# The first microseconds of an encoder trunk: copies of the row selectors queued on VectorE behind the first head's row parts, and mask transfers to device memory queued behind GpSimd's other masks

## The chip, the cores and the metric

One core of one Trainium2 chip runs the whole program. The metric is the device time of one execution in microseconds (us); a run's figure is the median of several executions, and the profile is of one further execution. TensorE (PE) multiplies matrices, VectorE (DVE), ScalarE (ACT) and GpSimd (POOL) work element by element, SyncE (SP) issues most of the DMA transfers. Each engine works through its own queue in order; it waits at the head of that queue until what the instruction needs is there.

## The reference

Two residual layers, each a token mixer and a squared-ReLU MLP; layer 0 mixes with a bidirectional gated DeltaNet of 8 heads, layer 1 with a bidirectional GLA of 4 heads. 512 tokens of width 1024. The change touches only the start of layer 0:

```python
def _mixer_gdn(h, w_in, conv_w, a_log, dt_bias, norm_g, w_out):
    proj = jnp.matmul(h, w_in).astype(F32)
    qkv = jax.nn.silu(_depthwise_conv(proj[..., :A_CONV_CH], conv_w.astype(F32)))
    z = proj[..., A_CONV_CH:A_CONV_CH + A_VW]
    ba = proj[..., A_CONV_CH + A_VW:].reshape(bn, s, 2, 2, A_HEADS)
    q = _l2norm(heads(qkv[..., :A_W], A_DK)) * (A_DK ** -0.5)
    k = _l2norm(heads(qkv[..., A_W:2 * A_W], A_DK))
    v = heads(qkv[..., 2 * A_W:], A_DV)
    beta = jax.nn.sigmoid(ba[:, :, 0]).transpose(2, 0, 3, 1)
    g = (-jnp.exp(a_log) * jax.nn.softplus(ba[:, :, 1] + dt_bias)).transpose(2, 0, 3, 1)
    o_f = _gated_delta_chunked(q, k, v, beta[0], g[0])
    o_b = _flip(_gated_delta_chunked(_flip(q), _flip(k), _flip(v), _flip(beta[1]), _flip(g[1])))
    ...
```

Within a chunk the delta rule needs `exp(gc[i] - gc[j])` for all pairs of rows i, j of the chunk (`gc` is the running sum of `g`), masked to one triangle per direction, and the inverse of a unit triangular matrix built from it.

## The kernel before

**Tiling.** The 512 tokens are four blocks of 128 (`NT` = 4), the width is eight blocks (`KT` = 8). Products keep fp32 accuracy by splitting each operand into a high and a low part: ScalarE casts the high part (`wh`, `xth`; L102), VectorE subtracts to get the low part (`wl`, `xtl`; L107), and TensorE does three products per block of the width (L128, L129, L130). A projection of one head (`pjk`, `pjq`, `pjv`, `pjz`) is thus 24 matmuls of 128x128 by 128x512. Weights come into three rotating buffers `wst`; the split parts also have three buffers.

**Stages.** `gates` projects the gate columns (`bap`) and the key of head 0 (`pjk`) as the first blocks of x arrive, after 42 transposes without use, then computes log decays on VectorE: a chain of small operations on tiles `gd`, `ge`, `gl`, `gy` (L1295 to L1313). `masks` has GpSimd build the constant masks. Then the heads run as a pipeline: each round gives head i-2 its recurrence (`recur`), head i-1 its solve (`solve`) and head i its projections (`project`).

**Head 0.** `project` ends each of k, q, v with a five-tap convolution (`conv`): one ScalarE product (L1418) and four VectorE operations (L1422). When k and q are done, ScalarE loads the table for SiLU, applies it to both (L1465), loads the former table again (L57), and TensorE transposes k, then q, into one bank (`ktp`, L1489), from which ScalarE takes sums of squares (`junk`, L1494). From their logarithm `lnr` and from `gc` VectorE forms the row parts `rw` and `rsp` (L1505, L1546, L1547), TensorE turns them into rows (`rtp`, L1550, copied to `rt`), and for head 0 alone `spread_by_products` spreads these rows over 128 partitions by a product with the two selectors `sel` (`ep`, L1560). A selector is a 4x128 tile; GpSimd makes both in `sf` (named `self`, L1181 to L1183) and VectorE casts them (L1187). Later heads spread their rows through device memory instead: SP fills the tile `E` with the masks `laterd` (L1470), and GpSimd's queue adds the rows (L1539). `laterd` is written once, by four transfers that GpSimd issues (L1194).

**What sets the order.** A scheduler at build time puts the instructions of each engine in an order, by estimated durations and by the order of the code; `issue_after(x)` places what is written under it behind instruction x. At run time the order of an engine is fixed. The tiles `yr`, `gl`, `self` and `E` of the heads take turns in the two buffers of tag "E", so head 1's `E` may be filled only when the selectors have been read from `self`.

Of the kernel before, what the change touches and what calls it, by code (L numbers as in the profile page):

```python
# [8 lines left out]
F32 = mybir.dt.float32  # L9
F32R = mybir.dt.float32r  # L10
# [3 lines left out]
ALU = mybir.AluOpType  # L14
# [3 lines left out]
P = 128  # L18
# [3 lines left out]
NT = S // P  # L22
# [884 lines left out]
class GlaHead:  # L907


    def __init__(self, c, pool, h, w_in, consts, masks, oth, otl):  # L910
        self.c, self.pool, self.h, (self.w_in, self.w_vr) = c, pool, h, w_in
        self.consts, self.masks, self.oth, self.otl = consts, masks, oth, otl
# [210 lines left out]
NEG = -1e30  # L1123


class GdnConst:
# [47 lines left out]
    def masks(self):  # L1174
        c, pool = self.c, self.pool
        G = c.nc.gpsimd
        self.idh = pool.tile([P, P], F16, name="idh", bufs=1)
        G.tensor_copy(self.idh, c.ident)

        sf = pool.tile([4, 2, P], F32, name="self", tag="E", bufs=2)  # L1180
        G.memset(sf, 0.0)  # L1181
        for s in range(2):
            G.affine_select(out=sf, in_=sf, compare_op=ALU.not_equal, fill=1.0, base=-2 * s,  # L1183
                            pattern=[[-1, 2], [0, P]], channel_multiplier=1)
        self.sel = [pool.tile([4, P], F32R, name=f"sel{d}", tag="vn", bufs=9) for d in range(2)]
        for d in range(2):
            c.nc.vector.tensor_copy(self.sel[d], sf[:, d, :])  # L1187

        self.after = later = pool.tile([P, 2, P], F32, name="later", bufs=1)
        for d in range(2):  # L1190
            self.tri(later[:, d, :], d, False, 0.0, NEG)
        self.later = self.dram.tile([P, 2, NT, P], F32, name="laterd", bufs=1)
        for n in range(NT):
            G.dma_start(self.later[:, :, n, :], later)  # L1194

        self.nd = pool.tile([P, P], F32, name="nd", bufs=1)
        G.tensor_scalar(self.nd, c.ident, -1.0, 1.0, ALU.mult, ALU.add)

        self.same4 = pool.tile([P, P], F16, name="same4", bufs=1)
        self.off = {}  # L1200
        prev = None
        for w in (4, 8, 16, 32):
            f = pool.tile([P, P], F32, name="blk", tag="cf", bufs=2)
            G.memset(f, 1.0)
            fv = f.rearrange("p (a b) -> p a b", b=w)
            G.affine_select(out=fv, in_=fv, compare_op=ALU.is_ge, fill=0.0, base=0,
                            pattern=[[-w, P // w], [0, w]], channel_multiplier=1)
            G.affine_select(out=fv, in_=fv, compare_op=ALU.is_ge, fill=0.0, base=w - 1,
                            pattern=[[w, P // w], [0, w]], channel_multiplier=-1)
            if w == 4:  # L1210
                G.tensor_copy(self.same4, f)
            else:
                m = pool.tile([P, NT, P], F16, name=f"off{w // 2}", bufs=1)
                G.tensor_tensor(m, f.unsqueeze(1).to_broadcast([P, NT, P]), prev.unsqueeze(1).to_broadcast([P, NT, P]),
                                ALU.subtract)
                self.off[w // 2] = m
            prev = f

        ic = pool.tile([P, P // 4, 4], F32, name="ic", tag="cf", bufs=2)
        G.tensor_copy(ic, c.ident.rearrange("p (b c) -> p b c", c=4))  # L1220
        n = P // 4
        while n > 1:
            n //= 2
            G.tensor_tensor(ic[:, :n, :], ic[:, :n, :], ic[:, n:2 * n, :], ALU.add)
        self.ic = pool.tile([P, 4], F16, name="icc", bufs=1)
        G.tensor_copy(self.ic, ic[:, 0, :])

    @contextlib.contextmanager
    def then(self):
# [164 lines left out]
class GdnHead:  # L1394
# [146 lines left out]

    def turn_rows(self, rw):

        c, V = self.c, self.c.nc.vector
        rs = c.small.tile([P, NT, 4], F32R, name="rsp", tag="rsp")
        V.tensor_copy(rs[:, :, 0:2], rw)  # L1546
        V.tensor_tensor(rs[:, :, 2:4], rw, rs[:, :, 0:2].bitcast(F32), ALU.subtract)  # L1547
        rtp = self.bank("rtp", tag="tp")
        for n in range(NT):
            c.nc.tensor.transpose(rtp[:4, n, :], rs[:, n, :].bitcast(F32), c.ident)  # L1550
        self.rt = self.pool.tile([4, S], F32R, name="rt0", tag="on", bufs=2)
        c.nc.scalar.copy(self.rt, rtp[:4, :, :].rearrange("p n i -> p (n i)"))
# [340 lines left out]
```

## Time and profile before

| what | value |
|---|---|
| median of 3 runs | 1319.1 us (1318.91 to 1319.72) |
| the profiled execution | 1320.66 us, its span 1319.0 us, mean granted TensorE clock 0.995 |
| busy: TensorE / VectorE / ScalarE / GpSimd | 1295.5 / 1105.9 / 803.8 / 136.5 us |
| DMA | 165.92 MB, mean 126 GB/s |

In the rows of a timeline the columns are start in us, duration in us, engine, line, operation, tile written from tiles read, shape, count; in brackets how long the engine stood idle before the row and what released it. Rows can overlap, since an engine starts one before the last has drained. The group and queue lines carry their own labels. SPq, POOLq and PEq are the queues' own steps, such as issuing a transfer.

### The profile page before, as it was taken

The page shows a single profiled execution, that of the slowest core. Times are in us where ns is not written, and L with a number is a line of the kernel's source. Part 1 is how long each engine was busy: PE and PEld are TensorE (multiplying, and loading weights), DVE is VectorE, ACT ScalarE, POOL GpSimd, SP SyncE. Part 2 cuts the span into 40 slices and gives each one's busy share as a digit, 9 for nine tenths or more (in the row PEclk, how much of TensorE's full clock was granted, in tenths as well). Part 3 has the DMA queues.
Part 4 walks back from the last instruction along what each step waited for, and adds up shares of the span by engine and source line. Part 5 has one row for each costly group of instructions (what it writes and reads, how often), then busy time and mean ns, then how long its engine had stood idle before and what let it go on. Part 6 is the DMA issues. An engine that isn't in the chain of part 4 may idle for free.

```text
span 1319.0 us, 22255 instructions
## 1 busy us (share of the span) xinstructions
PE 1295.5 (98%) x8608; PEld 1110.9 (84%) x8608; DVE 1105.9 (84%) x1789; ACT 803.8 (61%) x1598; POOL 136.5 (10%) x190
## 2 busy tenths in 40 slices
PE   9999999999999999999999999999999999999996
PEld 7778888788877899999998888888889899989985
DVE  6788889878868989989988787867879789899987
ACT  4567676777633666656667754554466566566656
POOL 6000000000001810101101100000001001101021
PEclk9899999999999999999999999999999999999998
DMA  5233223332422575476547521211216276556565
GB/s 198 81 112 97 62 84 98 97 97 75 134 84 95 179 155 191 116 213 169 147 152 160 154 81 63 81 48 64 97 65 224 80 208 161 143 176 134 172 142 143
DMA packets 47373, 165.92 MB, mean 126 GB/s; under 512 B 5875, under 2 KB 6307, under 8 KB 47267
## 3 DMA queue, kind: packets, MB, share of 16 engines
q1 hardware_dynamic: 33171, 114.52, 25.7%
q0 software_dynamic: 13984, 49.95, 18.6%
q8 instruction: 67, 1.10, 0.3%
q14 instruction: 39, 0.32, 0.1%
q10 hardware_dynamic: 112, 0.03, 0.0%
HBM read 125.00 MB, written 2.65 MB: 97 GB/s over the span
## 4 chain that ended last, share of the span: by engine, by line
PE 85%; DVE 5%; ACT 4%; DMA 2%; issue 2%; POOL 1%; SPq 0%; DVEq 0%; ACTq 0%; POOLq 0%
PE pjv L128 3%; PE pjv L129 3%; PE pjv L130 3%; PE pX L130 3%; PE pX L129 3%; PE pX L128 3%; PE m L1755 3%; PE fx L130 3%; PE fx L128 3%; PE fx L129 3%; PE fyz L128 2%; PE fyz L130 2%; PE fyz L129 2%; PE pj L130 2%; PE pj L129 2%; PE scp L1008 2%
## 5 line engine op out<-in xcount | busy, mean ns | idle before, releaser
L102 ACT CAST wh<-wst 128x1024 fp32r<-128x1024 f32 x152 | 159.6, 1050 | 107.4 <-PE fyz L129 27.9
L107 DVE TENSOR_TENSOR wl<-wst,wh 128x1024 fp32r<-128x1024 f32 x150 | 184.3, 1231 | 41.5 <-ACT wh L102 41.1
L107 DVE TENSOR_TENSOR w2l<-w2r,w2h 128x1024 fp32r<-128x1024 f32 x92 | 111.4, 1221 | 21.4 <-ACT w2h L102 21.4
L102 ACT CAST w2h<-w2r 128x1024 fp32r<-128x1024 f32 x94 | 98.4, 1048 | 42.3 <-DMA w2r<-w2r 25.1
L415 POOL DMA_DIRECT2D w2r<-w2r x56 | 47.9, 887 | 494.2 <-DVE w2l L107 278.8
L464 DVE TENSOR_TENSOR wst<-wst 128x512 f32<-128x512 f32 x120 | 80.0, 686 | 0.8
L102 ACT CAST ah<-h 128x1024 fp32r<-128x1024 f32 x56 | 58.8, 1050 | 30.2 <-PE pY L129 11.5
L107 DVE TENSOR_TENSOR al<-h,ah 128x1024 fp32r<-128x1024 f32 x56 | 68.3, 1220 | 6.6 <-ACT ah L102 6.6
L130 PE MATMUL pX<-w2h,al 128*128 128x512 f32 x168 | 66.3, 394 | 0.0
L129 PE MATMUL pX<-w2l,ah 128*128 128x512 f32 x168 | 65.9, 392 | 0.0
L128 PE MATMUL pX<-w2h,ah 128*128 128x512 f32 x168 | 65.5, 390 | 0.0
L128 PE MATMUL pjv<-wh,xth 128*128 128x512 f32 x128 | 54.8, 428 | 0.0
L130 PE MATMUL fyz<-xh,wl 128*128 128x256 f32 x192 | 53.5, 279 | 0.0
L130 PE MATMUL fx<-xth,wl 128*128 128x256 f32 x192 | 53.4, 278 | 0.0
L128 PE MATMUL fyz<-xh,wh 128*128 128x256 f32 x192 | 53.4, 278 | 0.0
L128 PE MATMUL fx<-xth,wh 128*128 128x256 f32 x192 | 53.2, 277 | 0.0
L130 PE MATMUL fx<-xh,wl 128*128 128x256 f32 x192 | 53.2, 277 | 0.0
L128 PE MATMUL fx<-xh,wh 128*128 128x256 f32 x192 | 53.2, 277 | 0.0
L129 PE MATMUL fyz<-xl,wh 128*128 128x256 f32 x192 | 53.2, 277 | 0.0
L129 PE MATMUL fx<-xtl,wh 128*128 128x256 f32 x192 | 53.1, 277 | 0.0
L129 PE MATMUL fx<-xl,wh 128*128 128x256 f32 x192 | 53.1, 277 | 0.0
L129 PE MATMUL pj<-xtl,wh 128*128 128x256 f32 (+1 forms) x160 | 52.0, 326 | 0.2 <-DVE xtl L194 0.2
(540 smaller groups left out, 4318.4 us busy)
## 6 DMA issues: line engine op xcount, KB each, us to landing
wst<-in_w SPq DMA_DIRECT2D x68, 512.0 KB, 4.6
w2r<-in_w SPq DMA_DIRECT2D x60, 512.0 KB, 4.5
w2r<-w2r POOLq DMA_DIRECT2D x56, 512.0 KB, 5.8
wst<-in_a_in SPq DMA_DIRECT2D x32, 512.0 KB, 4.2
wst<-in_b_vr SPq DMA_DIRECT2D x16, 512.0 KB, 3.4
wst<-in_a_out SPq DMA_DIRECT2D x8, 512.0 KB, 4.4
wst<-in_b_in SPq DMA_DIRECT2D x8, 512.0 KB, 3.5
wst<-in_b_out SPq DMA_DIRECT2D x8, 512.0 KB, 3.2
```

The source lines that it names most:

```text
L102: h = nc.scalar.copy(hi, src)
L107: self.halves = h, nc.vector.tensor_tensor(lo, src, hi.bitcast(F32), ALU.subtract)
L128: mm(ps, ah, bh, start=start, stop=False, **kw)
L129: mm(ps, ah, bl, start=False, stop=False, **kw)
L130: self.last_mm = mm(ps, al, bh, start=False, stop=stop, **kw)
L415: nc.gpsimd.dma_start(blocks[a + (q,)], blocks[b + (q,)], accum_op=ALU.add)
L464: plus = lambda a, b: V.tensor_tensor(a, a, b, ALU.add)
L1008: T.matmul(ps[:, n, :], kh[:, sl], qh[:, sl], start=True, stop=True)
L1755: T.matmul(ps[:, d, :], *ops(d), start=True, stop=True)
```

## The change

The making of `sf` and of the `later` masks moves to the end of `masks`, behind all other masks, and the four transfers to `laterd` are placed behind the last operation on `sf`. The two casts of the selectors leave `masks` and go to `turn_rows` of head 0, behind the second row part.

```diff
@@ masks
         self.idh = pool.tile([P, P], F16, name="idh", bufs=1)
         G.tensor_copy(self.idh, c.ident)
 
-        sf = pool.tile([4, 2, P], F32, name="self", tag="E", bufs=2)
-        G.memset(sf, 0.0)
-        for s in range(2):
-            G.affine_select(out=sf, in_=sf, compare_op=ALU.not_equal, fill=1.0, base=-2 * s,
-                            pattern=[[-1, 2], [0, P]], channel_multiplier=1)
-        self.sel = [pool.tile([4, P], F32R, name=f"sel{d}", tag="vn", bufs=9) for d in range(2)]
-        for d in range(2):
-            c.nc.vector.tensor_copy(self.sel[d], sf[:, d, :])
-
-        self.after = later = pool.tile([P, 2, P], F32, name="later", bufs=1)
-        for d in range(2):
-            self.tri(later[:, d, :], d, False, 0.0, NEG)
-        self.later = self.dram.tile([P, 2, NT, P], F32, name="laterd", bufs=1)
-        for n in range(NT):
-            G.dma_start(self.later[:, :, n, :], later)
-
         self.nd = pool.tile([P, P], F32, name="nd", bufs=1)
...
         G.tensor_copy(self.ic, ic[:, 0, :])
+
+        sf = pool.tile([4, 2, P], F32, name="self", tag="E", bufs=2)
+        G.memset(sf, 0.0)
+        for s in range(2):
+            made = G.affine_select(out=sf, in_=sf, compare_op=ALU.not_equal, fill=1.0, base=-2 * s,
+                                   pattern=[[-1, 2], [0, P]], channel_multiplier=1)
+        self.sf = sf
+
+        self.after = later = pool.tile([P, 2, P], F32, name="later", bufs=1)
+        for d in range(2):
+            self.tri(later[:, d, :], d, False, 0.0, NEG)
+        self.later = self.dram.tile([P, 2, NT, P], F32, name="laterd", bufs=1)
+        with c.tc.issue_after(made.ins):
+            for n in range(NT):
+                G.dma_start(self.later[:, :, n, :], later)
@@ turn_rows
-        c, V = self.c, self.c.nc.vector
+        c, V, g = self.c, self.c.nc.vector, self.g
+        g.sel = [self.pool.tile([4, P], F32R, name=f"sel{d}", tag="vn", bufs=9) for d in range(2)]
         rs = c.small.tile([P, NT, 4], F32R, name="rsp", tag="rsp")
         V.tensor_copy(rs[:, :, 0:2], rw)
-        V.tensor_tensor(rs[:, :, 2:4], rw, rs[:, :, 0:2].bitcast(F32), ALU.subtract)
+        lo = V.tensor_tensor(rs[:, :, 2:4], rw, rs[:, :, 0:2].bitcast(F32), ALU.subtract)
+        with c.tc.issue_after(lo.ins):
+            for d in range(2):
+                V.tensor_copy(g.sel[d], g.sf[:, d, :])
```

The scheduler then gives other orders on every engine up to the solve of head 0; from there on, and for the rest of the program, the orders are the same as before.

On VectorE, between the convolution of head 0's key and that of its query, the order before has the two casts of the selectors among the steps of the gate chain:

```order
L1422 SCALAR_TENSOR_TENSOR sil<-pjk,cw,sil 128x510
L1309 SCALAR_TENSOR_TENSOR gl<-gl,gd 128x128
L1187 CAST sel_298<-self 4x128
L1309 SCALAR_TENSOR_TENSOR gl<-gl,gd 128x128
L1187 CAST sel_299<-self 4x128
L1309 SCALAR_TENSOR_TENSOR gl<-gl,gd 128x128
L1422 SCALAR_TENSOR_TENSOR sil<-pjq,cw,sil 128x510
```

At the same place of the changed kernel (whose line numbers are one lower here) the query's convolution follows at once:

```order
L1421 SCALAR_TENSOR_TENSOR sil<-pjk,cw,sil 128x510
L1308 SCALAR_TENSOR_TENSOR gl<-gl,gd 128x128
L1421 SCALAR_TENSOR_TENSOR sil<-pjq,cw,sil 128x510
L1308 SCALAR_TENSOR_TENSOR gl<-gl,gd 128x128
L1421 SCALAR_TENSOR_TENSOR sil<-pjq,cw,sil 128x511
```

Both casts are gone from this place, and two of the gate chain's steps stand behind the query's convolution instead.

On VectorE of the changed kernel, at the row parts of head 0, the casts now stand behind `rsp`, and the splits of two weights of head 1 (its q and its v) stand ahead of `rw`; before, only the split of v stood there and that of q fourteen rows ahead of `rw`:

```order
L107 TENSOR_TENSOR wl<-wst,wh 128x1024
L1336 TENSOR_TENSOR tg<-lg,tot 128x64
L107 TENSOR_TENSOR wl<-wst,wh 128x1024
L1504 SCALAR_TENSOR_TENSOR rw<-lnr,gc 128x4x2
L1511 SCALAR_TENSOR_TENSOR cj<-lnr,lg 128x8
L1516 SCALAR_TENSOR_TENSOR kds<-lnr,tg 128x8
L1546 CAST rsp<-rw 128x4x2
L1521 TENSOR_TENSOR c_531<-lnr 128x4
L1547 TENSOR_TENSOR rsp<-rw,rsp 128x4x2
L1550 CAST sel_510<-self 4x128
L1550 CAST sel_511<-self 4x128
```

What moved here is the pair of casts, down to the place where the rows that they will be multiplied with are just being made.

On TensorE, in the projection of head 0's z, before, the transposes of k stand behind five whole blocks of the width (15 matmuls of `pjz`); these rows are the end of the fourth block, the fifth, the transposes and the start of the sixth:

```order
L129 MATMUL pjz<-xtl,wh 128x512
L130 MATMUL pjz<-xth,wl 128x512
L128 MATMUL pjz<-xth,wh 128x512
L129 MATMUL pjz<-xtl,wh 128x512
L130 MATMUL pjz<-xth,wl 128x512
L1489 MATMUL ktp<-ident,sil 128x128 x4
L128 MATMUL pjz<-xth,wh 128x512
```

In the changed kernel they stand behind 11 matmuls of `pjz`, inside the fourth block:

```order
L128 MATMUL pjz<-xth,wh 128x512
L129 MATMUL pjz<-xtl,wh 128x512
L1488 MATMUL ktp<-ident,sil 128x128 x4
L130 MATMUL pjz<-xth,wl 128x512
L128 MATMUL pjz<-xth,wh 128x512
```

The transposes moved four matmuls up. On GpSimd the four transfers to `laterd` were behind `nd` and ahead of the first `blk` mask; now they are the last thing ahead of head 1's rows. On SP the first filling of `E` stands one weight load earlier than before.

## The prediction

> **What bounds the kernel now.** I read the page first: busy shares, then the row of granted clocks, 40 equal slices of 33 us.
>
> ```profile
> span 1319.0 us, 22255 instructions
> PE 1295.5 (98%) x8608; PEld 1110.9 (84%) x8608; DVE 1105.9 (84%) x1789; ACT 803.8 (61%) x1598; POOL 136.5 (10%) x190
> PEclk9899999999999999999999999999999999999998
> ```
>
> TensorE is busy 98% of the span, so a change at the start is worth only what it gives TensorE: a wait removed, or a faster clock. The clock is low in the last slice, where the program drains, and in the second (33 to 66 us). The mean clock of 0.995 means 6.6 us lost in all: the drain's slice, at 0.8 to 0.9 of 33 us, has at least 3.3 of them. Next the waits of TensorE, longest first (us in total, times, longest):
>
> ```profile
> PE ktp L1489 <- ACT sil L1465: 3.1, 3, 2.7
> PE idle L1258 <- POOL ident masks.py:199: 1.5, 1, 1.5
> ```
>
> One wait stands out: the transposes of head 0's k wait 2.7 us for SiLU. The table by stretches (busy us of PE, PEld, DVE, ACT, POOL, then granted clock, DMA share, GB/s) puts wait and clock together:
>
> ```profile
> 32.00:36.00 4.00, 2.67 (x12) 1.85 (x10) 4.00 (x9) 1.05 (x2) 0.00 (x0) 1.00 0.01 2
> 36.00:40.00 4.00, 2.58 (x10) 2.17 (x11) 2.10 (x5) 3.96 (x8) 0.00 (x0) 0.80 0.64 164
> 40.00:44.00 4.00, 4.00 (x15) 3.46 (x14) 2.16 (x7) 1.51 (x6) 0.00 (x0) 0.50 0.24 98
> 44.00:48.00 4.00, 4.00 (x19) 3.22 (x18) 2.41 (x5) 2.16 (x12) 0.00 (x0) 0.85 0.14 31
> ```
>
> The clock falls to half just behind the wait and is lost for 4 x 0.20 + 4 x 0.50 + 4 x 0.15 = 3.4 us, which with the drain's is all that the run loses. So the wait costs twice. What it waited for is read backwards from three timelines, here in order of time:
>
> ```profile
> 26.48 0.69 ACT L1418 ACTIVATE sil<-pjq,cw 128x512 f32<-128x512 f32 x1
> 28.19 0.28 DVE L1309 SCALAR_TENSOR_TENSOR gl<-gl,gd 128x128 f32<-128x128 f32 x1
> 30.04 0.86 POOL L1183 TENSOR_SCALAR_AFFINE_SELECT self<-self 4x256 f32<-4x256 f32 x2
> 30.94 0.21 DVE L1187 CAST sel<-self 4x128 fp32r<-4x128 f32 x1 [2.47 <-POOL self L1183]
> 31.62 0.73 DVE L1422 SCALAR_TENSOR_TENSOR sil<-pjq,cw,sil 128x510 f32<-128x510 f32 x1
> 34.20 0.73 DVE L1422 SCALAR_TENSOR_TENSOR sil<-pjq,cw,sil 128x510 f32<-128x510 f32 x1
> 35.01 1.28 ACT L1465 ACT_TABLE_LOAD   x1 [2.95 <-DVE sil L1422]
> 36.30 1.06 ACT L1465 ACTIVATE sil<-sil 128x1024 f32<-128x1024 f32 x1
> 34.27 0.40 PE L130 MATMUL pjz<-xth,wl 128*128 128x512 f32 x1
> 37.41 0.66 PE L1489 MATMUL ktp<-ident,sil 128*128 128x128 f32 x4 [2.74 <-ACT sil L1465]
> ```
>
> VectorE stands 2.47 us at the cast of a selector that GpSimd has not made; behind it wait the query's convolution, the table load, SiLU and TensorE.
>
> **Part 1, the casts leave VectorE's row.** The query's product is done at 26.48 + 0.69 = 27.17, so the convolution can start when the gate step of 28.19 is over, at 28.47 instead of 31.62: 3.15 us earlier, and with it everything down to the transposes, 37.41 - 3.15 = 34.26. ScalarE is free for the table: the cast that stood ahead of it now stands behind the first sums of squares. TensorE comes to the transposes earlier too, four matmuls of `pjz` earlier. Warm, seven matmuls take the time from the first to the second of these rows, 0.23 us each:
>
> ```profile
> 47.25 0.40 PE L128 MATMUL pjk<-xth,wh 128*128 128x512 f32 x1
> 48.88 0.40 PE L129 MATMUL pjk<-xtl,wh 128*128 128x512 f32 x1
> 43.04 0.63 PE L128 MATMUL pjk<-xth,wh 128*128 128x512 f32 x1
> 43.47 0.63 PE L129 MATMUL pjk<-xtl,wh 128*128 128x512 f32 x1
> ```
>
> It is there at 34.27 + 0.23 - 0.92 = 33.58 and waits 0.7 us. In work done the gain is 3.15 - 0.92 = **2.2 us**; with the last 0.7 gone too it would be 2.9.
>
> **Part 2, the clock.** The next longest wait of the run, 1.5 us, and all shorter ones have no low clock behind them. A wait of 0.7 us should not either. In the low stretch a matmul takes 0.43 us (from the third to the fourth row above) instead of 0.23, that is 47% too much; with 3.4 us of clock lost the stretch is 6.8 us of half speed, and 0.47 x 6.8 = **3.2 us** go. Bounds: 0, if the clock falls all the same, and 3.4.
>
> [...]
>
> **Part 3, the row parts.** Once TensorE no longer crawls, what was hidden under the slow stretch could show. I replay the new orders with the durations of these rows.
>
> ```profile
> 40.06 0.47 PE L1326 MATMUL gcp<-gy,cum 128*128 128x32 f32 x2
> 41.62 0.77 PE L128 MATMUL pjz<-xth,wh 128*128 128x512 f32 x1
> 46.12 0.60 PE L1489 MATMUL ktp<-ident,sil 128*128 128x128 f32 x4
> 49.52 0.60 PE L1550 MATMUL rtp<-ident,rsp 128*4 128x128 f32 x4 [0.24 <-DVE rsp L1547]
> 52.53 0.50 PE L128 MATMUL pjq<-xth,wh 128*128 128x512 f32 x1
> 62.26 0.35 PE L1612 MATMUL hp<-icc,a 128*128 128x4 f16 x8
> 51.93 1.23 DVE L107 TENSOR_TENSOR wl<-wst,wh 128x1024 fp32r<-128x1024 f32 x1 [2.17 <-ACT wh L102]
> 39.15 0.28 ACT L1494 ACTIVATE junk<-ktp 128x128 f32<-128x128 f32 x1
> 56.07 0.73 DVE L1422 SCALAR_TENSOR_TENSOR sil<-pjk,cw,sil 128x510 f32<-128x510 f32 x1
> 58.59 0.41 DVE L1601 TENSOR_TENSOR a<-ath,same 128x512 f16<-128x512 f16 x1
> ```
>
> TensorE: transposes at 34.26 (0.42), ten matmuls, the gate sums `gcp` (1.56 us at half clock, so about 0.85), nine matmuls: it wants the transposes of q at 39.9. ScalarE, from the end of SiLU at 34.2: a table load (1.3), a copy (0.5), one convolution product (0.6), two weight casts (1.0 each) and four sums of squares (0.27 each), 5.5 us, and 0.3 us until the buffer of the second cast is free: the bank is free at 40.0, just in time.
>
> Before, TensorE then lost 49.52 - (48.88 + 0.23) = 0.4 us waiting for `rsp`, whose chain took 49.52 - 46.12 = 3.4 us from the transposes of q. In the new order 16 matmuls stand between them, 0.35 + 16 x 0.23 = 4.0 us, so `rtp` stands at 44.0 and the 0.4 us go. The split that now stands ahead of `rw` has to fit: VectorE has the gate sums at 37.9, three convolutions and small copies take it to 40.7, two splits of about 1.15 to 43.1, and `rw` to `rsp` 0.8 us more, 43.9. The casts, 2 x 0.21 us, stand behind `rsp`; the products that read them come only after the rows have been turned and copied, so they are hidden.
>
> From `rtp` to the row of 52.53 is 3.0 us before and after, and from there to `hp` 9.7: `hp` stands at 56.7. VectorE's last input to it follows from the first `qd`, at 47.8: ten operations of a convolution's length or less, started at most 0.66 us apart, one split of 1.15 and two `a` of 0.4, 8.5 us: 56.3, early by 0.4. So **0.4 us** gained in this part, with -0.6 as the other end (0.5 lost at the transposes of q and 0.5 at one of the other two places). Summed, parts 1 to 3 bring TensorE 5.8 us forward at the solve of head 0, from which on the orders agree.
>
> **Part 4, the transfers.** Before, four transfers leave GpSimd from 3.45 us, while the first blocks of x and weights come in. The queue row is that of the first 15 us.
>
> ```profile
> 3.45 3.04 POOL L1194 DMA_DIRECT2D laterd<-later  x4
> q0 software_dynamic: 192, 0.52, 8.8%
> 16.64 1.05 ACT L102 CAST wh<-wst 128x1024 fp32r<-128x1024 f32 x1 [1.10 <-DMA wst<-in_a_in]
> 17.97 1.05 ACT L102 CAST wh<-wst 128x1024 fp32r<-128x1024 f32 x1 [0.28 <-DMA wst<-in_a_in]
> 19.00 0.50 PE L130 MATMUL pjq<-xth,wl 128*128 128x512 f32 x1 [0.54 <-DVE wl L107]
> 19.55 1.07 PE L1286 MATMUL gtp<-sum,yr 64*128 64x32 f32 x8
> ```
>
> Their 0.52 MB take 8.8% of 16 engines over 15 us, 1.3 us of everything. The loads behind them may land up to 1.3 us earlier. ScalarE waited 1.10 and 0.28 us for two of them, and TensorE's rows at 19.00 and 19.55 hang on these casts, so up to 1.3 us come through; the gate chain on VectorE starts from the second, so the gain also moves the chain of part 1. The lower end is 0, if x is served ahead of these writes anyway. I take **1.0 us**, nearest to the 1.10 of the first cast. At their new place, behind 30.9 us, the transfers meet the next weight load, issued at about 33 and cast only after the rows have been turned, at about 45.7, twelve us later: hidden. The first reader of `laterd` stands on SP behind the splits that end at 43.1. If that cover were gone, the load behind it would be late by as much; it brings weights of head 2, which are wanted only in the next round. The masks that GpSimd now makes earlier or later are first read behind the row of 52.53 and cost nothing.
>
> **Sum.** 2.2 + 3.2 + 0.4 + 1.0 = 6.8 us. The profiled execution took 1320.66 us with a span of 1319.0, so it should come to 1313.9; it stands 1.6 us above the median of the runs, 1319.1. I take the same gain off the median: **1312.3 us**. The 1.6 us might partly be a low clock that lasts longer under the profiler; then the runs have less to gain, which the range holds.
>
> **Rivals.** *The low clock stays*, either from another cause or because the remaining 0.7 us suffices. For it: nothing shows what sets off the clock except that one occasion. Against it: it falls once in the run, right behind the one long wait. Then 2.2 + 0.4 + 1.0 = 3.6 go, 1315.5 us. [...]
>
> *The change does not do what it says*: the four transfers occupy GpSimd for 3.04 us from 30.9 on, and VectorE, whose convolution ends at 31.7, could be held by them as it was by the selector. The end of the convolution then falls near 34.7, against 34.93 before; wait and low clock remain, and only 1.0 + 0.2 us are won: 1317.9 us. Against it:
>
> ```profile
> 5.56 1.23 DVE L1248 TENSOR_TENSOR xtl<-xt,xth 128x1024 fp32r<-128x1024 f32 x1 [1.72 <-ACT xth L1247]
> ```
>
> This row began while the same transfers were being issued (3.45 to 6.49) and took what a subtraction of that size took at 51.93.
>
> *Slower*: the slow stretch gave VectorE and ScalarE 3.2 us to catch up. Without it the chain from the spread rows to `hp` decides. If it is later than 56.7 by x, TensorE waits x, and from about 2.7 us on the low clock comes back there, 3.2 us. With x = 7 that is 10.2 lost against 6.8 won: 1322.5 us; it is slower than before from x = 3.6 on, by more than can be told from no change from x = 6.2. Against it: the replay has the chain 0.4 us early, and no row in it is as long as this miss.
>
> **How the numbers follow.** Chances: forecast 0.80, low clock stays 0.11, does not do what it says 0.06, slower 0.03. The forecast's own range goes from 1310.6 to 1314.5: all upper ends are 2.9 + 3.4 + 0.4 + 1.3 = 8.0, 1311.1 us; with both 1.0 off in parts 3 and 4 and 0.2 elsewhere it is 4.6, 1314.5; half a us at the lower end is for the runs before, which spread over 0.8. The first rival at 1315.5 takes the range to 1315.8, so it is 1310.6 to 1315.8. A measurement of this kernel can tell about 0.2%, 2.6 us, from no change. Faster by more than that: 0.80 + 0.11 = 0.91; within it 0.06; slower 0.03.
>
> **What would show it.** Right: the query's convolution starts at 27.4 to 28.5, `ktp` with under 1 us of idle time ahead of it, a clock of 1.00 in every stretch from 32 to 48 us, `hp` near 55.5, and ScalarE's casts at 16.64 and 17.97 about 1 us earlier. Wrong: a clock under 1 behind `ktp`, a new wait of over 2 us at `ktp` of q, `rtp` or `hp`, or a selector cast with idle time ahead of it. What falls the prediction is any of these, or first loads that land no earlier together with new waits in the solve of head 0.

## The result and the profile after

| | before | after |
|---|---|---|
| median of 5 runs each, us | 1318.91 (1317.76 to 1319.72) | 1313.41 (1312.42 to 1313.65) |
| ratio, 95% interval | 1 | 0.9958 [0.9944, 0.9973] |
| the profiled execution, its span, us | 1320.66, 1319.0 | 1313.51, 1311.8 |

The medians differ by 5.5 us, the two profiled executions by 7.2. The forecast was 6.8, 1312.3 us. The page of the kernel after, its span, busy shares and granted clocks:

```profile
span 1311.8 us, 22252 instructions
PE 1292.4 (99%) x8608; PEld 1109.6 (85%) x8608; DVE 1105.7 (84%) x1789; ACT 803.4 (61%) x1598; POOL 134.0 (10%) x190
PEclk9999999999999999999999999999999999999998
```

The second slice is no longer low, and only the drain's is left. TensorE's waits after (us in total, times, longest):

```profile
PE idle L1257 <- POOL ident masks.py:199: 1.5, 1, 1.5
PE fyz L128 <- ACT h L523: 1.1, 2, 0.6
PE tp L190 <- DVE xt L276: 1.0, 3, 0.6
PE ktp L1488 <- ACT sil L1464: 0.8, 3, 0.5
```

`ktp` fell from the first place, with 2.7 us at once, to 0.5. The table by stretches after, in the columns used before (the sixth number behind the length is the granted clock):

```profile
32.00:36.00 4.00, 3.49 (x18) 2.64 (x17) 1.68 (x6) 3.96 (x7) 1.07 (x2) 1.00 0.73 230
36.00:40.00 4.00, 4.00 (x25) 3.36 (x24) 3.47 (x10) 3.45 (x11) 0.00 (x0) 1.00 0.00 0
40.00:44.00 4.00, 4.00 (x21) 3.16 (x20) 3.26 (x12) 2.38 (x13) 0.00 (x0) 1.00 0.44 135
44.00:48.00 4.00, 4.00 (x22) 3.00 (x21) 2.75 (x5) 3.19 (x5) 0.00 (x0) 1.00 0.71 264
```

All four are at 1.00, and TensorE stands idle only 0.51 us in them. The timelines after, engine by engine, of the rows on which the sum rested:

```profile
14.19 1.05 ACT L102 CAST wh<-wst 128x1024 fp32r<-128x1024 f32 x1 [1.17 <-DMA wst<-in_a_in]
16.73 1.05 ACT L102 CAST wh<-wst 128x1024 fp32r<-128x1024 f32 x1 [1.50 <-PE pjk L1270]
31.05 1.28 ACT L1464 ACT_TABLE_LOAD   x1 [4.64 <-DVE sil L1421]
27.43 0.27 DVE L1308 SCALAR_TENSOR_TENSOR gl<-gl,gd 128x128 f32<-128x128 f32 x1
27.63 0.73 DVE L1421 SCALAR_TENSOR_TENSOR sil<-pjq,cw,sil 128x510 f32<-128x510 f32 x1
30.24 0.74 DVE L1421 SCALAR_TENSOR_TENSOR sil<-pjq,cw,sil 128x510 f32<-128x510 f32 x1
42.78 0.34 DVE L1550 CAST sel<-self 4x128 fp32r<-4x128 f32 x2
30.12 2.95 POOL L1225 DMA_DIRECT2D laterd<-later  x4
```

The query's convolution follows the gate step with nothing between (27.63; before 31.62), and the table load moves from 35.01 to 31.05. The casts at their new place have no idle time ahead of them. GpSimd issues the four transfers from 30.12 to 33.07 while the last convolution of the query starts at 30.24 and takes 0.74 us, against 0.73 before. TensorE after:

```profile
1.53 7.34 PE L1257 MATMUL idle<-ident 128*128 128x128 f32 x42 [1.53 <-POOL ident masks.py:199]
18.83 1.07 PE L1285 MATMUL gtp<-sum,yr 64*128 64x32 f32 x8
33.46 0.66 PE L1488 MATMUL ktp<-ident,sil 128*128 128x128 f32 x4 [0.51 <-ACT sil L1464]
39.26 0.60 PE L1488 MATMUL ktp<-ident,sil 128*128 128x128 f32 x4
43.42 0.60 PE L1553 MATMUL rtp<-ident,rsp 128*4 128x128 f32 x4
56.17 0.35 PE L1615 MATMUL hp<-icc,a 128*128 128x4 f16 x8
```

Read against the rows of before: `gtp` 0.72 us earlier (19.55), the transposes of k 3.95 (37.41), those of q 6.86 (46.12), `rtp` 6.10 (49.52), `hp` 6.09 (62.26). No row from the transposes of q on has a new wait. Of their 6.86 us, 0.76 goes into the new order between them and `rtp`; `hp` has two more matmuls of projections ahead of it than before, 0.47 us of work, so TensorE is 6.6 us ahead there. Of the 7.2 us of the profiled pair some 0.6 thus came behind `hp`, where the orders agree.

### The profile page after: what moved, and what is told of

It is laid out like the page before. It is cut to its first block, busy times and chain, and to the rows that moved or that the text cites. A ratio compares the mean times of both kernels' runs of the same rounds, so it can differ in the third digit from the quotient of the medians.

```text
span 1311.8 us, 22252 instructions
## 1 busy us (share of the span) xinstructions
PE 1292.4 (99%) x8608; PEld 1109.6 (85%) x8608; DVE 1105.7 (84%) x1789; ACT 803.4 (61%) x1598; POOL 134.0 (10%) x190
## 4 chain that ended last, share of the span: by engine, by line
PE 83%; DVE 7%; ACT 5%; DMA 3%; issue 2%; POOL 0%; DVEq 0%; ACTq 0%; POOLq 0%
PE pjv L128 3%; PE pjv L129 3%; PE pjv L130 3%; PE pX L130 3%; PE pX L129 3%; PE m L1758 3%; PE pX L128 3%; PE fx L130 3%; PE fx L128 3%; PE fx L129 3%; PE pj L129 2%; PE fyz L128 2%; PE pj L130 2%; DMA w2r<-w2r 2%; PE scp L1008 2%; PE pj L128 2%
```

## The experiments

Each ran beside runs of the kernel before on the same chip. "Clock" is the mean over the runs of the mean granted TensorE clock.

| run | median us (range, runs) | ratio to before [95%] | clock |
|---|---|---|---|
| before, as it is | 1318.84 (1317.88 to 1321.86, 12) | 1.0002 [0.9990, 1.0013] | 0.9958 |
| the whole change | 1313.59 (1311.43 to 1314.14, 8) | 0.9959 [0.9944, 0.9973] | 0.9970 |
| casts moved alone | 1314.45 (1312.96 to 1316.08, 11) | 0.9965 [0.9953, 0.9977] | 0.9967 |
| selectors made early | 1314.34 (1313.82 to 1315.20, 5) | 0.9965 [0.9951, 0.9978] | 0.9970 |
| selectors made early, transfers moved | 1314.15 (1312.31 to 1314.87, 5) | 0.9967 [0.9955, 0.9980] | 0.9970 |
| transfers moved alone | 1318.69 (1316.53 to 1322.77, 12) | 1.0006 [0.9993, 1.0018] | 0.9949 |
| transfers moved alone, again | 1318.54 (1317.28 to 1320.72, 11) | 1.0001 [0.9991, 1.0011] | 0.9955 |
| selectors inside the chain of `ic` | 1316.54 (1315.81 to 1317.34, 11) | 0.9979 [0.9970, 0.9988] | 0.9966 |
| selectors ahead of `ic` | 1316.33 (1314.52 to 1318.60, 11) | 0.9981 [0.9972, 0.9990] | 0.9970 |
| a longer wait | 1322.25 (1320.91 to 1324.79, 9) | 1.0030 [1.0019, 1.0040] | 0.9946 |
| 32 transposes at the start | 1313.71 (1311.94 to 1314.26, 5) | 0.9957 [0.9945, 0.9970] | 0.9972 |

The medians of the kernel before beside them were 1318.58 (30 runs; beside the first three rows of the table and the transfers alone), 1319.06 (21; beside the early selectors alone, the two shorter waits and the 32 transposes) and 1318.80 (19; beside the other three).

### The kernel before, unedited

> The kernel before, unchanged, to see how its executions differ. My theory: every execution has the wait of 2.5 to 3 us ahead of the transposes of head 0's k and a half-speed stretch behind it, but that stretch may be one or two periods long, so the mean clock is between 0.995 and 0.997 and the times spread by up to 2 us around 1319. Rival: the stretch is always 6.8 us, the clock always 0.995, and the profiled execution was slow for another reason.

It ran as before. Its trace (TensorE's row, then the table by stretches) has the same wait and half as much low clock:

```profile
37.89 1.12 PE L1489 MATMUL ktp<-ident,sil 128*128 128x128 f32 x4 [2.77 <-ACT sil L1465]
36.00:40.00 4.00, 2.11 (x7) 1.91 (x8) 2.57 (x5) 3.96 (x7) 0.00 (x0) 0.73 0.51 150
40.00:44.00 4.00, 4.00 (x20) 3.35 (x19) 1.66 (x6) 1.96 (x6) 0.00 (x0) 0.84 0.34 113
```

Lost are 4 x 0.27 + 4 x 0.16 = 1.7 us of clock, where the profiled execution of the prediction had lost 3.4. The same program with the same wait thus loses now one, now the other. At `hp` this execution stands 1.06 us ahead of the first (61.20 against 62.26 us) although its `gtp` came 0.47 later (20.02 against 19.55), so the second half of that stretch had cost 1.5 us. Yet the two took 1320.52 and 1320.66 us in all: behind `hp`, in the same order, this one lost 0.9 us; the largest step is at a wait of 0.5 us for `fyz` near 1232 us that the first does not have. Its 12 runs spread wider than expected, with clocks of 0.993 to 0.997. In stretches of half a us, of this run and then of the first profile, the first and the last that are partly low show where it starts and ends; between them all stand at 0.50:

```profile
37.50:38.00 0.50, 0.11 (x1) 0.11 (x2) 0.50 (x1) 0.48 (x2) 0.00 (x0) 0.85 0.69 66
...
41.00:41.50 0.50, 0.50 (x5) 0.44 (x3) 0.00 (x0) 0.00 (x0) 0.00 (x0) 0.73 0.62 254
```

```profile
38.00:38.50 0.50, 0.50 (x4) 0.42 (x3) 0.13 (x1) 0.50 (x1) 0.00 (x0) 0.87 0.95 352
...
45.00:45.50 0.50, 0.50 (x3) 0.36 (x3) 0.50 (x3) 0.06 (x1) 0.00 (x0) 0.80 0.00 0
```

A clock of 0.85 over half a us is 0.15 us at half speed, so the low stretch started at 37.85; 0.73 is 0.27 us, so it ended at 41.27, 3.42 us later. In the first profile the same reading gives 38.37 to 45.20, 6.83 us, twice that.

### The casts moved, the transfers where they were

Lines in brackets stand for code of the change above.

```diff
-        (making of sf, casts of sel, behind idh)
+        (making of sf behind icc)
@@ turn_rows
-        V.tensor_tensor(rs[:, :, 2:4], rw, rs[:, :, 0:2].bitcast(F32), ALU.subtract)
+        lo = V.tensor_tensor(rs[:, :, 2:4], rw, rs[:, :, 0:2].bitcast(F32), ALU.subtract)
+        with c.tc.issue_after(lo.ins):
+            for d in range(2):
+                V.tensor_copy(g.sel[d], g.sf[:, d, :])
```

> Only the selectors' casts and their source move; the four transfers stay at the start. Engines' orders as in the changed kernel but for GpSimd. Theory (wait of the casts and the clock behind it): 4.0 to 5.5 us faster than before, 1313.5 to 1315, clock 1.00 from 32 to 48 us, under 1 us of wait ahead of the transposes of k, the third and fourth weight casts of ScalarE still near 16.6 and 18. Rival (the earlier loads make most of the gain): at most 2.5 us faster, 1316.5 or more.

4.1 us below the runs of before beside it (1318.58). In its trace the clock is 1.00 from 32 to 48 us, and the wait is down to 0.52 us; `gtp` is as late as in the kernel before (19.55 and 20.02 in its two profiles):

```profile
20.06 1.07 PE L1284 MATMUL gtp<-sum,yr 64*128 64x32 f32 x8
34.74 0.66 PE L1487 MATMUL ktp<-ident,sil 128*128 128x128 f32 x4 [0.52 <-ACT sil L1463]
```

So most of the gain is the casts'.

### The transfers moved, the casts where they were

```diff
-        (later masks and their four transfers, ahead of nd)
+        (later masks behind icc)
+        with c.tc.issue_after(made.ins):
+            for n in range(NT):
+                G.dma_start(self.later[:, :, n, :], later)
```

`made` is the last operation on `sf`. It ran twice.

> Only the four transfers and the making of their masks move behind GpSimd's other masks; the casts stay in front of the query's convolution. Orders as before but for GpSimd. Theory: 0 to 1.3 us faster, 1317.6 to 1319; the wait of about 2.5 us at the cast and the low clock stay; the third and fourth weight casts of ScalarE come 1 to 2.5 us earlier. Rival (the loads make most of the gain): 3 us or more faster, 1316 or less.

> The transfers alone a second time (first: 1318.69 us, ratio 1.0006). If the low clock swallows their gain: ratio 1.000 again, and a mean clock 0.0005 or more below that of the kernel before. If the first was chance and they are worth 1 us by themselves: ratio 0.9992.

No change in either. In the trace of the second run the loads do come earlier, and then the wait and the low clock follow (ScalarE, TensorE, the stretch behind the wait):

```profile
14.64 1.05 ACT L102 CAST wh<-wst 128x1024 fp32r<-128x1024 f32 x1 [1.07 <-DMA wst<-in_a_in]
18.23 1.07 PE L1287 MATMUL gtp<-sum,yr 64*128 64x32 f32 x8
36.06 1.01 PE L1490 MATMUL ktp<-ident,sil 128*128 128x128 f32 x4 [2.71 <-ACT sil L1466]
36.00:40.00 4.00, 3.94 (x15) 3.36 (x16) 0.74 (x3) 2.98 (x8) 0.00 (x0) 0.57 0.82 255
```

`gtp` is 1.3 us and `ktp` 1.35 us earlier than in the first profile of before, but that is not seen in the medians. Nor is it lost on the way in the traces: with one unit of low clock in all three, `hp` stands at 59.49 and 59.41 in these two profiles and at 61.20 in the kernel before, run again. Sorted by clock, 8 of these 23 runs have a mean of 0.994 or less, against 9 of 82 of the kernel before; the other 15 average 1318.0 us, the other 73 of before 1318.7. So some 0.7 us may be there, eaten by a low clock that lasts longer more often. The limit of 0.994 was chosen after the runs, and why the low clock should last longer is not shown.

### The whole change, again

> The changed kernel, unchanged, beside the two halves on the same chip. Theory: the halves add up, so its gain equals that of the casts alone plus that of the transfers alone within 0.7 us, near 5.5 us. Rival: the halves overlap (both shorten the same wait), and the sum of the two is over 1 us more than the whole.

1313.59, 0.9 us below the casts alone: that would be the transfers' share where no low clock is left, but the two intervals overlap by more than that. The halves alone give 4.1 and -0.1, the whole 5.0: the sum is 1.0 short of the whole, which is neither the theory nor the rival.

### A shorter wait, in two sizes

Nothing moves but the making of the selectors on GpSimd; VectorE, ScalarE and TensorE keep the orders of before. `made` is the last operation on `sf`.

```diff
 # ahead of ic
-        G.tensor_copy(ic, c.ident.rearrange("p (b c) -> p b c", c=4))
+        with c.tc.issue_after(made.ins):
+            G.tensor_copy(ic, c.ident.rearrange("p (b c) -> p b c", c=4))
 # inside the chain of ic
-            G.tensor_tensor(ic[:, :n, :], ic[:, :n, :], ic[:, n:2 * n, :], ALU.add)
+            with c.tc.issue_after(made.ins) if n <= 4 else contextlib.nullcontext():
+                G.tensor_tensor(ic[:, :n, :], ic[:, :n, :], ic[:, n:2 * n, :], ALU.add)
```

> The kernel before, with the selectors' source made on GpSimd ahead of the sums for `ic` (2.1 us of work) instead of behind them; all other engines keep the order of before. The cast on VectorE then waits about 0.4 us instead of 2.5 and the transposes of k about 0.8 instead of 2.9. Theory (the wait itself and a half clock that only a long wait brings): 2.1 us from the wait and 1.7 us of clock, 3.4 to 4.2 us faster, about 1314.8, mean clock of the runs as in the changed kernel, 0.997. [...]

> The same with the source made after the first two of the five sums: about 1.1 us earlier than before, so the transposes of k wait about 1.8 us. It asks how long a wait must be to bring the half clock. Theory: a wait shorter than 2.9 us brings it less often; 1.1 us from the wait plus 0.8 to 1.7 of clock, 1316 to 1316.8, mean clock 0.9962 to 0.997. Rival (any wait of over 1 us brings it as before): 1.1 us faster, 1317.5, mean clock 0.9956.

Inside the chain, TensorE's row and the two stretches behind it:

```profile
37.11 0.66 PE L1490 MATMUL ktp<-ident,sil 128*128 128x128 f32 x4 [1.66 <-ACT sil L1466]
36.00:40.00 4.00, 2.89 (x19) 2.63 (x20) 1.79 (x4) 3.97 (x8) 0.00 (x0) 1.00 0.69 210
40.00:44.00 4.00, 4.00 (x20) 3.17 (x20) 3.99 (x11) 2.81 (x12) 0.00 (x0) 1.00 0.13 52
```

In this execution a wait of 1.66 us is followed by no low clock. The wait is 1.1 us shorter than the 2.77 of the kernel before, the time 2.5 us less (1319.06 to 1316.54), so about 1.4 us are left for the clock; the mean clock, 0.9966 against 0.9961 in the runs beside it, accounts for 0.7 of them. Two of the 11 runs have a clock of 0.995, which no run of the changed kernel has, so a low stretch in some of them is not ruled out.

Ahead of `ic`, with a wait of 0.83 and no low clock in the trace, the mean clock came out as the theory had it (0.9970), but the time did not: 2.7 us were gained, not 3.4 to 4.2, only 0.6 more than the 2.1 that were expected of the wait alone. In its trace the missing part is there at `hp`: 57.42 us, 3.8 earlier than in the kernel before, run again, and 1.5 earlier than inside the chain. So it was not lost on the way to `hp`; why the medians show less is open.

### A longer wait

```diff
-                G.tensor_tensor(m, f.unsqueeze(1).to_broadcast([P, NT, P]), prev.unsqueeze(1).to_broadcast([P, NT, P]),
-                                ALU.subtract)
+                for _ in range(2 if w > 8 else 1):
+                    G.tensor_tensor(m, f.unsqueeze(1).to_broadcast([P, NT, P]), prev.unsqueeze(1).to_broadcast([P, NT, P]),
+                                    ALU.subtract)
```

> The kernel before with two of GpSimd's mask subtractions (about 1.3 us each) done twice, ahead of the selectors; the orders of all other engines are as before. VectorE then stands some 5.1 us at the selector cast and TensorE some 5.3 us at ktp, 2.6 us longer than before. If a wait costs its length and sets off one low stretch whatever its length: 1318.8 + 2.6 = 1321.4 us, ratio 1.0020, and a mean clock as before, 0.9956. If a longer wait also brings a longer low stretch (two periods of 3.4 us in place of one): 1.6 us more, 1323.0 us, ratio 1.0032, mean clock 0.9943. If TensorE's wait were not what the end hangs on: no change.

3.45 us slower. VectorE's and TensorE's rows, then the stretches:

```profile
33.92 0.22 DVE L1187 CAST sel<-self 4x128 fp32r<-4x128 f32 x1 [4.64 <-POOL self L1183]
40.39 1.12 PE L1490 MATMUL ktp<-ident,sil 128*128 128x128 f32 x4 [5.50 <-ACT sil L1466]
36.00:40.00 4.00, 0.00 (x0) 0.00 (x0) 4.00 (x9) 2.01 (x2) 0.00 (x0) 0.93 0.00 2
40.00:44.00 4.00, 3.61 (x12) 3.04 (x12) 1.07 (x3) 3.31 (x8) 0.00 (x0) 0.50 0.74 235
44.00:48.00 4.00, 4.00 (x15) 3.52 (x14) 2.35 (x7) 1.34 (x4) 0.00 (x0) 0.50 0.07 28
48.00:52.00 4.00, 4.00 (x17) 3.21 (x17) 2.22 (x5) 1.85 (x10) 0.00 (x0) 0.79 0.17 47
```

The wait is 2.7 us longer than in the first two profiles of before, and the median rises by 0.75 more. Lost are 4 x (0.07 + 0.50 + 0.50 + 0.21) = 5.1 us of clock, that is 10.2 us at half: three times 3.4. The end does hang on this wait, and the longer one brought more low clock (mean 0.9946 against 0.9957 beside it); the time lies between the first two expectations.

### The selectors made early, with and without the transfers

Here `sel` doesn't depend on GpSimd's late masks at all: the source tiles no longer share the buffers of tag "E", so that VectorE casts them at 14.66 us.

```diff
-        sf = pool.tile([4, 2, P], F32, name="self", tag="E", bufs=2)
+        sf = [pool.tile([4, P], F32, name=f"self{d}", tag="vn", bufs=9) for d in range(2)]
...
-            c.nc.vector.tensor_copy(self.sel[d], sf[:, d, :])
+            c.nc.vector.tensor_copy(self.sel[d], sf[d])
```

> Another way to the same end: the selectors' source lies in two buffers that are free at the start (tag of the recurrence's tiles), so that GpSimd makes it at 3 us and VectorE casts it at its old place in the code, without waiting; transfers at their old place. TensorE and ScalarE have the order of the changed kernel. Theory (what counts is that VectorE doesn't wait, not where the casts stand): as the casts alone, 1314 to 1315 us. Rival (the new place of the casts matters): over 1 us from that.

The same time as the casts alone, 1314.34 and 1314.45: what counts is that VectorE doesn't stand, not where the casts went. Then the later masks and the transfers were moved as well, behind `icc`:

> The kernel of the early selectors (1314.34 us, ratio 0.9965) with the later masks and their four transfers behind all other masks, and nothing else. If the transfers are worth 0.9 us wherever the low clock is already gone, as the difference of 1314.45 and 1313.59 between the casts alone and the whole change says: 1313.4 us, ratio 0.9959, and ScalarE's second early weight cast and TensorE's gtp 1 us or more earlier than with the selectors alone. If that difference was chance: 1314.4 us, ratio 0.9965. In both no wait of a us at ktp and a clock of 1.00 up to 48 us.

0.2 us less in the median, not 0.9, and against the runs of before beside each no gain at all (4.7 us below them both times). In the profiles `gtp` moves from 20.17 to 18.65 us and `hp` from 57.06 to 55.99. This version is no faster than the change.

### Fewer transposes at the start

Where the changed kernel's second early cast waits for TensorE (`pjk`, the row of 16.73 above), 32 transposes in place of 42 should let the products start earlier.

```diff
-            for i in range(42):
+            for i in range(32):
```

> The changed kernel with 32 instead of 42 transposes without use at the start (work left out that the output doesn't need). In its profile the first product started at 7.8 to 8.6 us though its operands were there at 6.8, and the first loads land 2.4 us earlier than before. Theory: the transposes now cover the earlier loads, and 10 fewer let 0.6 to 1.3 us more through, 1312.3 to 1313. Rival (the clock needs them, or loads still bind): within 0.4 us of 1313.5, or slower because the first products run at half speed.

No gain. TensorE's timeline:

```profile
1.54 5.52 PE L1257 MATMUL idle<-ident 128*128 128x128 f32 x32 [1.54 <-POOL ident masks.py:199]
33.84 0.66 PE L1488 MATMUL ktp<-ident,sil 128*128 128x128 f32 x4 [1.40 <-ACT sil L1464]
```

TensorE begins its products 1.8 us earlier than after the change (6.82 against 8.62; 0.7 of it because its transposes came to full speed earlier, as the last section shows) and gives it back at `ktp`, where it waits 1.40 us in place of 0.51. Up to there the loads and VectorE's chain set the pace, not TensorE's start: ScalarE's cast at 16.67 us waits 0.29 for a load, and the query's convolution starts at 27.99, against 27.63 after the change.

## Why the prediction was right, and which term was mis-sized

**The mechanism held.** The cast that VectorE stood at, the query's convolution behind it, SiLU, the wait at the transposes and the low clock behind it are one chain. Shortened (1.66, 0.83, 0.52 us) the wait left no low clock in the profiles; lengthened (5.50) it brought more of it (10.24 us, against 3.41 to 6.83 with a wait of 2.7); with the wait taken away, the same gain came (1314.34 and 1314.45 us) whether the casts changed their place or not.

**Part 1, 2.2 us: held.** `ktp` was to be 3.15 us earlier through this part, and 0.7 us idle; it is 3.95 earlier, 0.72 of which is there at `gtp` already, so 3.2, with 0.51 idle.

**Part 2, 3.2 us: the mechanism right, the size twice too large.** The step that failed is "with 3.4 us of clock lost the stretch is 6.8 us of half speed, and 0.47 x 6.8": it took the length from one execution, in which the stretch was two units of 3.41 us. In the three other profiles with a wait of 2.7 us it was one unit, 0.47 x 3.41 = 1.6 us of work. Some executions of the kernel before may have none: 17 of the 82 have a mean clock of 0.997 or 0.998, as the changed kernel has. Over the runs the mean clock rises from 0.9958 (82 of the kernel before) to 0.9970 (8 after), 0.0012 x 1319 = 1.6 us; the run with a wait of 1.66 us leaves 1.4 for the clock by its time, 0.7 by its mean clock. With 1.6 the sum is 2.2 + 1.6 + 0.4 + 1.0 = 5.2 us, measured were 5.5 and, a second time, 5.0; that it fits so well is in part luck, since the 1.0 is not borne out (part 4). The prediction had named this case, a low clock that lasts longer in the profiled execution, and kept it in the range only. In the profiled pair, where the two units do go, 2.2 + 3.2 + 0.4 and the 0.7 of `gtp` make 6.5, and TensorE is 6.6 us ahead at `hp`: for that execution the sum was right, for the median it was not. One support of this part was misread: the wait of 1.5 us, said to have no low clock behind it, stands at the start of the program, where the clock's row reads 1.00 but the transposes start 0.213 us apart at first and 0.109 later (last section). That waits of 0.45 to 1.66 us at `ktp` had a clock of 1.00 behind them is shown by the profiles of the runs, not by that row.

**Part 3, 0.4 us: held.** The transposes of q, `rtp` and `hp` have no idle time ahead of them, where `rtp` had 0.24 us before. `hp` stands at 56.17, 6.1 us earlier; foreseen was 55.5. Parts 1 to 3 by the corrected size are 2.2 + 1.6 + 0.4 = 4.2 us, and the casts alone gave 4.1.

**Part 4, 1.0 us: not resolved.** The loads do land earlier: `gtp` stands at 18.2 to 18.8 us in all six profiles with the transfers moved and at 19.5 to 20.3 in all seven without, and `hp` comes 1.1 to 1.8 us earlier in the pairs that differ in the transfers and have the same low clock. The first of the two early casts even came 2.45 us earlier (14.19 against 16.64), more than the 1.3 that the queue's share had allowed; the second kept 1.2 of it, since in the changed kernel it waits for TensorE's products, which had begun 1.2 us later behind transposes that took 7.34 us in place of 6.11. But the medians give 0.9 us on top of the casts, nothing on top of the early selectors, and -0.1 and 0.3 alone. All that they bear out is a gain between nothing and about 1 us.

**The rivals.** The low clock did not stay, and a wait of 1.66 us had none behind it in the profile that has it; waits of 2.71 to 2.77 us had a low clock behind them in all four profiles that have them. GpSimd's transfers did not hold VectorE (the row of 30.24 beside that of 30.12), and the chain to `hp` was in time.

## What to carry to other kernels

The wait of TensorE cost more than its length here, since the granted clock fell to 0.50 behind it: by the estimate above 1.6 us of work on top of the 2.2 of part 1. Price the two apart, and price the second by the mean clock of several runs, since one profiled execution shows only one draw of its length (6.83 us in one profile of the kernel before, 3.42 in the other). To tell whether a low clock is owed to a wait, shorten the wait on the engine that causes it, with all other orders kept; that is a change of a few words here. Read the profiles of a pair at the first row from which the orders agree, and not only at their ends: from `hp` on, profiles with the same order of matmuls took 1254.5 to 1256.4 us (six of them) and 1256.3 to 1257.6 us (seven), spreads larger than the gain in question in part 4. And a gain seen at an early row of one trace, as that of the transfers, is not yet one of the program.

## What was unexpected of the hardware

**The low clock came in units.** The stretches at 0.50 lasted 3.42 (the kernel before, again), 3.41 and 3.42 (transfers alone), 6.83 (before) and 10.24 us (the longer wait): one, two and three times 3.41. They began 2.7 to 3.7 us after TensorE had gone idle with a wait of 2.7 us, and 4.6 us after with the wait of 5.5. With TensorE idle for 1.66 us none began in the one profile that has it.

The units of the five traces also differ in what they held. Whether that decides between one and two of them no run tests. A unit was followed by another where it held the whole of the gate sums `gcp`, eight narrow products, or 0.9 us of idle time. In the first profile of before these sums run from 40.06 to 41.62 us, inside the unit that ends at 41.78. A unit was the last where it held wide products and transposes and at most three of the eight. The kernel before, run again, has them just behind the end of its one unit at 41.27; the longer wait has them inside its second unit, 42.88 to 46.29, behind a first one in which TensorE still stood idle for 0.9 us:

```profile
41.33 0.30 PE L1326 MATMUL gcp<-gy,cum 128*128 128x32 f32 x2
43.86 0.47 PE L1327 MATMUL gcp<-gy,cum 128*128 128x32 f32 x2
```

**The start varied by itself, and the clock's row does not show it.** The 42 transposes at the start took 6.11 us in the first profile and 6.4 to 7.6 in the others. In each profile they start 0.213 us apart and from some moment on 0.109. That moment is 4.24 us in the first profile, 6.76 after the change, 4.9 to 7.4 in the others, and only there does the trace's record of the clock begin; the 1.00 in the views ahead of it stands for no record. Two rows of equal length, before and after the change, with 12 transposes and with 6:

```profile
4.74 1.47 PE L1258 MATMUL idle<-ident 128*128 128x128 f32 x12
4.79 1.49 PE L1257 MATMUL idle<-ident 128*128 128x128 f32 x6
```

The 2.52 us more at half the rate are 1.23 us of work, so the products that began 1.2 us later after the change owe that to the execution, not to the change. In the five profiles with a low stretch it began nine or ten times 3.413 us behind this moment (34.13 us in the first profile, 30.72 in the kernel before, run again). Since it lasted one, two or three times 3.41 us, its end too lies a whole number of these behind this moment in all five. The moment lies elsewhere in each execution, and with it the work that falls into the stretch. In the run with 32 transposes the earlier end of them did not reach the end of the program: products 1.8 us earlier, and a ratio of 0.9957 against 0.9959.
